# Expert outputs summed from gathered rows, with tokens on partitions, in place of a dense product over all experts

## The chip, the cores and the metric

One core of a Trainium2 chip runs the whole program; the other cores are idle. The metric is the device time of that core in microseconds (us). The kernel before takes 2015.12 us, the median of two runs (2014.29 and 2015.94).

## The reference, cut to what matters

The program is two transformer blocks, one after the other, on 256 tokens of width 1024 in float32. The first block ends with a product-key expert layer (`peer`). It scores 2 x 128 keys in each of 8 heads, takes the best 16 of each half, adds them pairwise, keeps the 16 best pairs, and so chooses 8 x 16 = 128 of 16,384 experts for each token, with a softmax gate for each. An expert is one row of `expert_u` and one row of `expert_v`:

```
u = expert_u[ii]                                   # 128 rows of 1024 for each token
h = jnp.einsum('tkd,td->tk', u, xx).astype(f32)
a = (jax.nn.gelu(h) * gg).astype(x.dtype)
return jnp.einsum('tk,tkd->td', a, expert_v[ii])   # sum over the token's 128 experts
```

The result is added to the residual and normalised. A context norm and the second block (a feed-forward, retention, a Fourier branch, another feed-forward) follow.

## The kernel before, in words

Activations stand with features on the 128 partitions and the 256 tokens along the free axis. A weight comes as a **unit** of 128 x 1024 float32 (512 KB): SP loads it into one of three `raw` buffers, ACT rounds it to `whi` (L108), DVE computes the rest `wlo` (L109), and PE makes three matmuls for each product (L245 to L247). `Emit.run` goes through a list of items, fetches units three ahead, and calls each item in that order; instructions of an engine run in the order in which the items emit them. Items of kind "e" use no weight.

The expert layer has these stages:

- **U stage.** The activations of all 16,384 experts for all tokens are computed densely, in 128 units `pu[b]` (`expert_u`): 24 matmuls, a Gelu on ACT (L1256), and a write of the 128 x 256 result to a DRAM tensor `uD` from the POOL queue (L1257). The choice of the experts (`topk`, `pick`, `gates`) runs on DVE beside the first 64 units.
- **Gate matrix G.** In units 64 to 122 the sparse gates are spread into a dense matrix of 16,384 experts by 256 tokens that stays in SBUF: `gbuild` builds one-hot matrices on DVE, 512 matmuls of 128 x 128 place them (L1243, L1244), and 64 ACT instructions copy them out (L1248).
- **V stage.** In 128 units `pv[b]` (`expert_v`) the gated activations multiply all rows of `expert_v`. For each pair of units POOL loads `early` from `uD` (L1353), DVE multiplies by G (L1383), ACT and DVE split the product into `ah` and `al`, and PE makes 24 matmuls into four accumulating banks `acc`.
- Beside the V stage run eleven `ada` steps: POOL loads a row of 512 KB (L102) and DVE takes its products (L1004). The context norm runs there too. `open_pd` loads the residual `h` back from the tensor `hD` (1 MB) from the POOL queue, two units before the end, and `done_c` adds the four banks to it. The next unit on PE is the context's part of the feed-forward, and then the part that reads `y`, made of the sum.

POOL's DMAs take eight completion semaphores in turn (DMASW0 to DMASW7), so that a DMA waits for the one that stands eight places ahead of it on POOL to have landed.

Of the kernel before, what the change touches and what calls it, by code (L numbers as in the profile page):

```python
# [14 lines left out]
U16 = mybir.dt.uint16  # L15
AF = mybir.ActivationFunctionType
# [11 lines left out]
GSCALE = 16384.0  # L28
# [6 lines left out]
TKE, GB0, GB1 = 63, 64, 58  # L35

NE = 7
# [13 lines left out]
class Emit:  # L51


    def __init__(self, nc, raw, split, ahead_raw, ahead_split):
        self.nc, self.raw, self.split = nc, raw, split
        self.ahead_raw, self.ahead_split = ahead_raw, ahead_split
        self.row, self.ahead_row, self.row_end = None, 0, 0
        self.late, self.soon = [], []

# [27 lines left out]
    def run(self, items, begin=None):  # L87
# [6 lines left out]
        def fetch():  # L94
# [5 lines left out]
            while nr < min(self.row_end, ur + self.ahead_row):  # L100
                rowt[nr] = self.row(nr)
                (nc.scalar if nr < self.ahead_row else nc.gpsimd).dma_start(out=rowt[nr], in_=rows[nr])  # L102
                nr += 1
# [95 lines left out]
def body(ctx, tc, I, out):  # L199
# [40 lines left out]
    uD = dram.tile([P, P, T], F32, name="uD")  # L240
# [784 lines left out]
    i1T = state.tile([P, T], F16, name="i1T")  # L1025
    i2T = state.tile([P, T], F16, name="i2T")
    ghT = state.tile([P, T], F16, name="ghT")
    glT = state.tile([P, T], F16, name="glT")
# [145 lines left out]
    def gates(t):  # L1174

        def a():
            pb = B["p"]
            v = B["vals", t]
            B["ge"] = pb.tile([P, 4, P], F32, name="ge", tag="cand", bufs=1)
            e = B["ge"][:, 0, :].rearrange("p (h k) -> p h k", h=8)  # L1180
# [4 lines left out]
        def b():  # L1185
# [5 lines left out]
            dve.tensor_scalar(out=rc, in0=rc, scalar1=GSCALE, scalar2=None, op0=ALU.mult)  # L1191
            dve.tensor_tensor(out=e, in0=e, in1=rc.unsqueeze(2).to_broadcast([P, 8, 16]), op=ALU.mult)
            e2 = e.rearrange("p h k -> p (h k)")
            h16 = pb.tile([P, P], F16, name="gh16", tag="gh16", bufs=1)
            dve.tensor_copy(h16, e2)
            h32 = B["ge"][:, 1, :]
            dve.tensor_copy(h32, h16)
            l32 = B["ge"][:, 2, :]
            dve.tensor_tensor(out=l32, in0=e2, in1=h32, op=ALU.subtract)
            B["hl"] = (h32, l32)  # L1200

        def c():
            h32, l32 = B["hl"]
            ps = bankB()
            for n, src in enumerate((B["x", 0, t], B["x", 1, t], h32, l32)):
                pe.matmul(ps[:, n * P:n * P + P], src, ident, start=True, stop=True)

            def g():
                for n, dst in enumerate((i1T, i2T, ghT, glT)):
                    dve.tensor_copy(dst[:, t * P:t * P + P], ps[:, n * P:n * P + P])  # L1210
            em.later(g)

        return [(0.5, [("e", None, a)]), (1.5, [("e", None, b)]), (2.0, []), (1.5, [("e", None, c)])]

    NG = 8

    def gbuild(g):

        ts = slice(g * NG, g * NG + NG)
        box = {}  # L1220

        def one_hot():
            pb = B["p"]

            def of(t):

                return t[:, ts].rearrange("p (g t) -> p g t", g=4).unsqueeze(2).to_broadcast([P, 4, P, 2])

            keys = iota.unsqueeze(1).to_broadcast([P, 4, P, 2])
            p1, p2, ph = [pb.tile([P, 4, P, 2], F16, name=n, tag=n, bufs=2) for n in ("p1", "p2", "ph")]  # L1230
            dve.tensor_tensor(out=p1, in0=keys, in1=of(i1T), op=ALU.is_equal)
            dve.tensor_tensor(out=p2, in0=keys, in1=of(i2T), op=ALU.is_equal)
            dve.tensor_tensor(out=ph, in0=p1, in1=of(ghT), op=ALU.mult)
            dve.tensor_tensor(out=p1, in0=p1, in1=of(glT), op=ALU.mult)
            box["t"] = (p2, p1, ph)

        def place(g4):
            p2, p1, ph = box["t"]
            ps = bankB()
            for i in range(4):  # L1240
                o = ps[:, i * P:i * P + P]
                k, t = 2 * g4 + i // 2, i % 2
                pe.matmul(o, p2[:, k, :, t], ph[:, k, :, t], start=True, stop=False)  # L1243
                pe.matmul(o, p2[:, k, :, t], p1[:, k, :, t], start=False, stop=True)  # L1244
            ps3 = ps.rearrange("p (t i) -> p t i", t=4)
            t0 = g * NG + 4 * g4
            o3 = B["G"][:, :, t0:t0 + 4].rearrange("p i t -> p t i")
            em.later(lambda: act.activation(out=o3, in_=ps3, func=AF.Copy, scale=1.0 / GSCALE))  # L1248

        return ("e", None, one_hot), ("e", None, lambda: place(0)), ("e", None, lambda: place(1))  # L1250

    def expert_u(b):

        def ev(ps):
            u = B["pu"].tile([P, T], F32, name="act", tag="act", bufs=2)
            act.activation(out=u, in_=ps[:, :T], func=AF.Gelu_apprx_tanh)  # L1256
            pool.dma_start(out=uD[:, b, :], in_=u)  # L1257
# [55 lines left out]
    gb = {}  # L1313
# [3 lines left out]
    gb[GB0][0:0] = [E(em.flush), E(lambda: open_g())]  # L1317
    gb.setdefault(GB0 + GB1 - 4, []).append(E(lambda: load_early(0)))
    gb[GB0 + GB1 + 3] += [E(em.flush), E(lambda: open_e()), E(lambda: gated(0))]
    gb[GB0 + GB1 + 4] = [E(lambda: ready1(0)), E(em.flush)]  # L1320
    gb[GB0 + GB1 + 5] = [E(lambda: ready1(1))]
# [5 lines left out]
    def open_g():  # L1327

        Bx.close()
        g = Gx.enter_context(tc.tile_pool(name="g", bufs=1))  # L1330
        B["G"] = g.tile([P, P, T], F32, name="G")
        B["pu"] = Gx.enter_context(tc.tile_pool(name="pu", bufs=1))
        C["e", 0] = B["pu"].tile([P, 2, T], F32, name="early0")
        B["p"] = Cgx.enter_context(tc.tile_pool(name="pg", bufs=1))

    def open_e():

        Cgx.close()
        B["pe"] = Gx.enter_context(tc.tile_pool(name="pear", bufs=NE - 1))
        for n in range(1, NE):  # L1340
            load_early(n)

    def part(a, n):

        return B["G"][:, a:a + n, :]
# [4 lines left out]
    def load_early(n):  # L1350
        if n > 0:
            C["e", n] = B["pe"].tile([P, 2, T], F32, name="early", tag="early")
        pool.dma_start(out=C["e", n], in_=uD[:, 2 * n:2 * n + 2, :])  # L1353

    def open_rows():
        K["cs"] = [flat(part(16 + 4 * n, 4)) for n in range(2)]
        K["junk"] = flat(part(24, 4))

    def load_ctx(n):
        pool.dma_start(out=part(40 + 4 * n, 4), in_=I["ctx"][:, 4 * n:4 * n + 4, :])  # L1360

    def load_rows():
        em.rows(lambda n: flat(part(28 + 4 * (n % 3), 4)), 2, ADA_C)
# [3 lines left out]
    def ready(b, a):  # L1367
        ah, al = apair()
        split(a, ah, al)
        C["a", b] = (ah, al)  # L1370

    def ready1(b):
        n = b // 2
        ready(b, C["e", n][:, b % 2, :])
        if b % 2 == 0:
            em.later(lambda: gated(n + 1))
        elif 0 < n and n + NE - 1 < 64:
            load_early(n + NE - 1)

    def gated(n):  # L1380

        if n < 64:
# [717 lines left out]
```

## Time and profile before

| | |
|---|---|
| median of the runs shown | 2015.12 us |
| the profiled execution | 2017.51 us, its span 2015.8 us |
| PE busy | 1990.5 us (99%) |
| DVE, ACT, POOL busy | 1397.2, 1015.9, 152.8 us |
| bytes moved by DMA | 393.18 MB, mean 195 GB/s |
| U stage, V stage (from PE in order of time) | some 248 to 659 us, 659 to 1025 us |

A busy PE is not a PE at its peak, since matmuls overlap: what one costs is the distance between the starts of two, not the duration in its row. The tables by stretch say how busy each engine and the DMA engines are in a stage; the groups say what ended an engine's idle time; the order of time shows distances.

### The profile page before, as it was taken

The page shows a single profiled execution, that of the slowest core. Times are in us where ns is not written, and L with a number is a line of the kernel's source. Part 1 is how long each engine was busy: PE and PEld are TensorE (multiplying, and loading weights), DVE is VectorE, ACT ScalarE, POOL GpSimd, SP SyncE. Part 2 cuts the span into 40 slices and gives each one's busy share as a digit, 9 for nine tenths or more (in the row PEclk, how much of TensorE's full clock was granted, in tenths as well). Part 3 has the DMA queues.
Part 4 walks back from the last instruction along what each step waited for, and adds up shares of the span by engine and source line. Part 5 has one row for each costly group of instructions (what it writes and reads, how often), then busy time and mean ns, then how long its engine had stood idle before and what let it go on. Part 6 is the DMA issues. An engine that isn't in the chain of part 4 may idle for free.

```text
span 2015.8 us, 37798 instructions
## 1 busy us (share of the span) xinstructions
PE 1990.5 (99%) x15348; PEld 1909.2 (95%) x15348; DVE 1397.2 (69%) x2282; ACT 1015.9 (50%) x1510; POOL 152.8 (8%) x296
## 2 busy tenths in 40 slices
PE   9999999999999999999999999999999999999998
PEld 8899999999999999999998888899989999999998
DVE  7668788877676666698876776578654556478555
ACT  6555545456666444545563333345644445346444
POOL 0000011111112101111000001010000000000000
PEclk9999999999999999999999999999999999999999
DMA  7655576766667777887764656677633334455664
GB/s 243 196 162 191 175 226 223 233 197 184 183 184 223 244 235 246 275 293 256 220 221 141 196 194 222 198 236 263 191 123 97 111 107 133 136 172 170 192 185 124
DMA packets 110094, 393.18 MB, mean 195 GB/s; under 512 B 14103, under 2 KB 14487, under 8 KB 109536
## 3 DMA queue, kind: packets, MB, share of 16 engines
q1 hardware_dynamic: 85968, 310.55, 48.8%
q0 software_dynamic: 22944, 77.52, 11.7%
q8 instruction: 120, 1.97, 0.4%
q10 hardware_dynamic: 1008, 2.70, 0.4%
q14 instruction: 54, 0.44, 0.1%
HBM read 371.84 MB, written 18.87 MB: 194 GB/s over the span
## 4 chain that ended last, share of the span: by engine, by line
PE 94%; DVE 2%; DMA 1%; ACT 1%; issue 1%; SPq 0%; ACTq 0%; DVEq 0%; POOLq 0%
PE wk L245 18%; PE wk L246 18%; PE wk L247 18%; PE acc L246 10%; PE acc L245 10%; PE acc L247 10%; PE acc L416 2%; PE acc L417 2%; PE acc L418 2%; DVE wlo L109 1%; PE wk L1243 1%; DMA raw<-w_dram 1%; PE wk L1244 1%; ACT whi L108 0%; ACT G L1248 0%
## 5 line engine op out<-in xcount | busy, mean ns | idle before, releaser
L109 DVE TENSOR_TENSOR wlo<-raw,whi 128x1024 fp32r<-128x1024 f32 x587 | 716.9, 1223 | 507.9 <-ACT whi L108 505.9
L108 ACT CAST whi<-raw 128x1024 fp32r<-128x1024 f32 x587 | 614.7, 1048 | 698.3 <-PE wk L246 338.3
L245 PE MATMUL wk<-nhi,whi 128*128 128x256 f32 (+1 forms) x1744 | 497.1, 285 | 10.3 <-ACT G L1248 10.3
L247 PE MATMUL wk<-nhi,wlo 128*128 128x256 f32 (+1 forms) x1744 | 491.7, 282 | 0.3 <-DVE wlo L109 0.3
L246 PE MATMUL wk<-nlo,whi 128*128 128x256 f32 (+1 forms) x1744 | 489.8, 281 | 0.0
L246 PE MATMUL acc<-al,whi 128*128 128x256 f32 x1376 | 387.9, 282 | 0.1
L247 PE MATMUL acc<-ah,wlo 128*128 128x256 f32 x1376 | 387.7, 282 | 0.0
L245 PE MATMUL acc<-ah,whi 128*128 128x256 f32 x1376 | 387.7, 282 | 0.0
L245 PEld LDWEIGHTS wk<-nhi,whi 128*128 128x128 f32 x1744 | 328.6, 188 | 12.6 <-ACT G L1248 11.7
L246 PEld LDWEIGHTS wk<-nlo,whi 128*128 128x128 f32 x1744 | 329.6, 189 | 0.6 <-issue 0.5
L247 PEld LDWEIGHTS wk<-nhi,wlo 128*128 128x128 f32 x1744 | 329.4, 189 | 0.6 <-DVE wlo L109 0.5
L246 PEld LDWEIGHTS acc<-al,whi 128*128 128x128 f32 x1376 | 259.2, 188 | 1.3 <-DVE al L377 0.5
L245 PEld LDWEIGHTS acc<-ah,whi 128*128 128x128 f32 x1376 | 259.3, 188 | 0.9
L247 PEld LDWEIGHTS acc<-ah,wlo 128*128 128x128 f32 x1376 | 259.3, 188 | 0.0
L246 PE MATMUL wk<-nxl,whi 128*128 128x512 f32 (+1 forms) x544 | 188.5, 346 | 0.0
L245 PE MATMUL wk<-nxh,whi 128*128 128x512 f32 (+1 forms) x544 | 188.2, 346 | 0.0
L247 PE MATMUL wk<-nxh,wlo 128*128 128x512 f32 (+1 forms) x544 | 187.3, 344 | 0.0
L376 ACT CAST ah<-early 128x256 fp32r<-128x256 f32 x128 | 52.1, 407 | 170.2 <-PE acc L247 163.8
L247 PEld LDWEIGHTS wk<-nxh,wlo 128*128 128x128 f32 x544 | 102.2, 188 | 13.2
L245 PEld LDWEIGHTS wk<-nxh,whi 128*128 128x128 f32 x544 | 102.1, 188 | 13.0
L246 PEld LDWEIGHTS wk<-nxl,whi 128*128 128x128 f32 x544 | 102.1, 188 | 11.8
L1257 POOL DMA_DIRECT2D uD<-act x128 | 69.1, 540 | 393.6 <-ACT act L1256 326.0
(534 smaller groups left out, 3215.5 us busy)
## 6 DMA issues: line engine op xcount, KB each, us to landing
raw<-pu_dram SPq DMA_DIRECT2D x128, 512.0 KB, 3.8
raw<-pv_dram SPq DMA_DIRECT2D x128, 512.0 KB, 4.3
row<-ada_dram POOLq DMA_DIRECT2D x59, 512.0 KB, 4.7
raw<-f13a_dram SPq DMA_DIRECT2D x44, 512.0 KB, 3.6
raw<-f2a_dram SPq DMA_DIRECT2D x44, 512.0 KB, 4.2
raw<-f13b_dram SPq DMA_DIRECT2D x44, 512.0 KB, 3.6
raw<-w_dram SPq DMA_DIRECT2D x41, 512.0 KB, 3.9
uD<-act POOLq DMA_DIRECT2D x128, 128.0 KB, 3.9
```

Of the source, the lines that this page charges most:

```text
L108: nc.scalar.copy(hi, r)
L109: nc.vector.tensor_tensor(out=lo, in0=r, in1=hi, op=ALU.subtract)
L245: pe.matmul(o, whi, xhi, start=start, stop=False)
L246: pe.matmul(o, whi, xlo, start=False, stop=False)
L247: pe.matmul(o, wlo, xhi, start=False, stop=stop)
L376: act.copy(hi, src)
L416: pe.matmul(o, xh[:, k, ts], hi[:, sl], start=k == 0, stop=False)
L417: pe.matmul(o, xh[:, k, ts], lo[:, sl], start=False, stop=False)
L418: pe.matmul(o, xl[:, k, ts], hi[:, sl], start=False, stop=k == KD - 1)
L1243: pe.matmul(o, p2[:, k, :, t], ph[:, k, :, t], start=True, stop=False)
L1244: pe.matmul(o, p2[:, k, :, t], p1[:, k, :, t], start=False, stop=True)
L1257: pool.dma_start(out=uD[:, b, :], in_=u)
```

## The change

The matrix G, its one-hot matrices and the dense product with `expert_v` go. The result is summed with tokens on partitions instead, in two halves t of 128 tokens. `gates` computes two tables of numbers per half: `idx` (which expert) and `el` (where in `uD` the activation of that expert for that token lies). For each half and each k of 128 there is a **slot**: one indirect DMA (`row`) fetches for each of the 128 tokens the row of its k-th expert from `expert_v` (512 KB in 128 pieces of 4 KB), and one indirect DMA (`element`) fetches its activation (128 pieces of 4 bytes). For an even k DVE multiplies the row by the gated activation and adds it to `o`; for an odd k ACT makes a diagonal matrix of the activations and PE adds its product with the row in two banks, by two matmuls of full float32. Elements are fetched 32 slots ahead, rows 14 slots ahead, in 16 buffers; the first 14 rows are fetched in the U stage. `back` turns the sums around into `acc` by 16 matmuls. The `ada` rows, the context and the conditioning vectors of this stage are now loaded from the SP queue.

```diff
-TKE, GB0, GB1 = 63, 64, 58
-NE = 7
+TKE = 64
+BEHIND, NROW, AHEAD = 14, 16, 32
...
-    uD = dram.tile([P, P, T], F32, name="uD")
+    uD = dram.tile([P * P, T], F32, name="uD")
...
         def c():
...
+            dve.scalar_tensor_tensor(out=f[0], in0=B["x", 0, t], scalar=float(P), in1=B["x", 1, t], op0=ALU.mult,
+                                     op1=ALU.add)
+            dve.tensor_copy(B["idx", t], f[0])
+            dve.tensor_scalar(out=f[1], in0=f[0], scalar1=float(T), scalar2=None, op0=ALU.mult)
+            dve.tensor_scalar(out=f[1], in0=f[1], scalar1=tok[:, t:t + 1], scalar2=None, op0=ALU.add)
+            dve.tensor_copy(B["el", t], f[1])
...
-    for g in range(T // NG):
-        for n, it in enumerate(gbuild(g)):
-            gb.setdefault(GB0 + g * GB1 // 31 + (0, 2, 3)[n], []).append(it)
...
+    gb = {TKE + 2: [E(em.flush), E(lambda: open_g())]}
+    for n in range(BEHIND):
+        gb[TKE + 4 + 3 * n] = [E(lambda n=n: row(n))]
...
+    def row(n):
+        t, k = divmod(n, P)
+        r = held["r", n] = B["rp"].tile([P, D], F32, name="erow", tag="erow")
+        pool.indirect_dma_start(out=r, out_offset=None, in_=I["pv"].rearrange("a b d -> (a b) d"),
+                                in_offset=at_(B["idx", t], t, k), bounds_check=P * P - 1)
+
+    def element(n):
+        t, k = divmod(n, P)
+        if k % 16 == 0:
+            held["a", n // 16] = B["p"].tile([P, 16], F32, name="ea", tag="ea", bufs=4)
+        pool.indirect_dma_start(out=held["a", n // 16][:, k % 16:k % 16 + 1], out_offset=None,
+                                in_=uD.rearrange("e t -> (e t)").unsqueeze(1), in_offset=at_(B["el", t], t, k),
+                                bounds_check=P * P * T - 1)
+
+    def use(n):
+        t, k = divmod(n, P)
+        a = held["a", n // 16]
+        if k % 16 == 0:
+            dve.tensor_tensor(out=a, in0=a, in1=B["gate", t][:, k:k + 16], op=ALU.mult)
+        r, a, o = held.pop(("r", n)), a[:, k % 16:k % 16 + 1], B["o", t]
+        if k == 0:
+            dve.tensor_scalar(out=o, in0=r, scalar1=a, scalar2=None, op0=ALU.mult)
+        elif k % 2 == 0:
+            dve.scalar_tensor_tensor(out=o, in0=r, scalar=a, in1=o, op0=ALU.mult, op1=ALU.add)
+        else:
...
+            d = B["p"].tile([P, P], F32, name="diag", tag="diag", bufs=4)
+            act.mul(d, ident, a)
+            for i in range(2):
+                pe.matmul(B["po"][i], d, r[:, i * 512:i * 512 + 512], start=k == 1, stop=k == P - 1)
+        if k == P - 1:
+            for i in range(2):
+                oi = o[:, i * 512:i * 512 + 512]
+                dve.tensor_tensor(out=oi, in0=oi, in1=B["po"][i], op=ALU.add)
+
+    def slot(n):
+        if n == 0:
+            for m in range(AHEAD):
+                element(m)
+        if n + AHEAD < 2 * P:
+            element(n + AHEAD)
+        if n + BEHIND < 2 * P:
+            row(n + BEHIND)
+        use(n)
...
+    def back():
+        accp.b = [bankA() for _ in range(4)]
+        for d in range(KD):
+            for t in range(2):
+                pe.matmul(accp.o(d)[:, t * P:t * P + P], B["o", t][:, d * P:d * P + P], ident, start=True, stop=True)
...
+    for n in range(2 * P):
+        items += beside.pop(n, []) + [E(lambda n=n: slot(n))]
+    assert not beside
+    items += [E(back), E(open_pd), E(done_c), E(em.flush)]
```

POOL, where the U stage ends and the V stage begins, before: writes of the activations and loads of `early` for a pair of units (128x512) alternate.

```order
L1257 DMA uD<-act 128x256 [waits DMASW1_49,Activation_49]
L1353 DMA early<-uD 128x512 [waits DMASW2_49,DVE_49,PE_49]
L1353 DMA early<-uD 128x512 [waits DMASW3_49]
...
L1257 DMA uD<-act 128x256 [waits DMASW4_49,Activation_49]
L1353 DMA early<-uD 128x512 [waits DMASW5_49,DVE_49]
L1353 DMA early<-uD 128x512 [waits DMASW6_49,DVE_49]
```

The same place in the changed kernel, where `ea` are the activations of 16 slots and `erow` is a row buffer:

```order
L1210 DMA uD<-act 128x256 [waits DMASW2_49,Activation_49]
L1210 DMA uD<-act 128x256 [waits DMASW3_49,Activation_49]
L1302 DMA ea<-uD,el_181 128x1 [waits DMASW4_49,DMASW5_49,DMASW3_49,DMASW6_49,DMASW2_49,DMASW7_49,DMASW1_49,DMASW0_49]
L1302 DMA ea<-uD,el_181 128x1 x7
L1302 DMA ea<-uD,el_181 128x1 [waits DMASW4_49]
...
L1295 DMA erow<-pv_dram,idx_180 128x1024 [waits DMASW5_49]
L1302 DMA ea<-uD,el_181 128x1 [waits DMASW6_49]
L1295 DMA erow<-pv_dram,idx_180 128x1024 [waits DMASW7_49]
L1302 DMA ea<-uD,el_181 128x1 [waits DMASW0_49]
L1295 DMA erow<-pv_dram,idx_180 128x1024 [waits DMASW1_49,DVE_49]
```

The first element now stands behind the landing of every write to `uD`. Behind it are 33 elements in a row, and then one row and one element in turn, to the end of the stage.

PE, from the last unit of the U stage to the first of the feed-forward, in the changed kernel (`cq` belongs to the context norm):

```order
L248 MATMUL wk<-nhi,wlo 128x256
L1322 MATMUL wk<-erow,diag 128x512 x212
L260 MATMUL wk<-cq_5424,ones 128x256 x2
L1322 MATMUL wk<-erow,diag 128x512 x44
L1354 MATMUL acc<-ident,o_5418 128x128
...
L1354 MATMUL acc<-ident,o_5419 128x128
L246 MATMUL wk<-nhi,whi 128x256
```

256 matmuls of 512 columns and 16 of 128 stand where 3,072 of 256 columns stood.

## Rows read from the trace of the kernel before

**Rows 1.** Page, part 2: the span in 40 slices of 50.4 us.
```profile
PEclk9999999999999999999999999999999999999999
DMA  7655576766667777887764656677633334455664
```

**Rows 2.** Busy time by stretch: second half of the U stage, then the V stage.
```profile
core 0: us, PE busy (x) PEld busy (x) DVE busy (x) ACT busy (x) POOL busy (x), PEclk, DMA share, GB/s
434.00:659.00 225.00, 214.74 (x2031) 210.90 (x2030) 153.34 (x191) 144.82 (x192) 37.47 (x70) 1.00 0.64 194
659.00:1025.00 366.00, 365.91 (x3078) 365.40 (x3078) 279.37 (x387) 189.05 (x280) 43.37 (x81) 1.00 0.78 253
```

**Rows 3.** PE in order of time (start, duration): the V stage's first matmul, and the first after it.
```profile
658.95 0.28 PE L245 MATMUL acc<-ah,whi 128*128 128x256 f32 x1
...
1024.99 0.28 PE L245 MATMUL wk<-nhi,whi 128*128 128x256 f32 x1
```

**Rows 4.** PE groups of 434 to 659 us: busy, mean ns, idle before.
```profile
L245 PE MATMUL wk<-nhi,whi 128*128 128x256 f32 x508 | 147.2, 290 | 10.3 <-ACT G L1248 10.3
```

**Rows 5.** PE in order of time: one placing (eight matmuls) between two units.
```profile
630.74 0.23 PE L1243 MATMUL wk<-ph,p 128*128 128x128 f16 x1
...
631.18 0.36 PE L245 MATMUL wk<-nhi,whi 128*128 128x256 f32 x1
631.39 0.28 PE L246 MATMUL wk<-nlo,whi 128*128 128x256 f32 x1
```

**Rows 6.** POOL groups of the whole span: busy, mean ns, idle before.
```profile
L1353 POOL DMA_DIRECT2D early<-uD x64 | 34.3, 537 | 277.1 <-DVE al L377 277.1
L612 POOL IOTA iota<- 128x256 f16 x1 | 1.5, 1512 | 0.4 <-POOLq L2086 0.4
```

**Rows 7.** Tile uD: its writes (ns min/median/max), issue to landing of all its DMAs.
```profile
L1257 POOL DMA_DIRECT2D uD<-act x128: 539/539/548, 252.0 to 662.2; - x128
...
DMA to landing us min/median/max: 1.9/3.9/7.8
```

**Rows 8.** POOL in order of time: six loads back to back.
```profile
647.38 3.19 POOL L1353 DMA_DIRECT2D early<-uD  x6
```

**Rows 9.** DMA of the V stage: slices, queue (packets, MB, share), issues (landing).
```profile
GB/s 230 230 237 232 236 223 227 235 238 236 223 227 246 222 293 270 278 308 216 348 226 295 295 298 283 291 278 301 280 295 217 237 223 241 215 220 207 177 201 364
...
q1 hardware_dynamic: 18268, 66.50, 54.9%
...
G<-ada_dram POOLq DMA_DIRECT2D x11, 512.0 KB, 6.6
raw<-f13a_dram SPq DMA_DIRECT2D x4, 512.0 KB, 9.2
...
G<-cc_dram POOLq DMA_DIRECT2D x2, 512.0 KB, 7.1
```

**Rows 10.** DVE groups of the V stage.
```profile
L109 DVE TENSOR_TENSOR wlo<-raw,whi 128x1024 fp32r<-128x1024 f32 x128 | 156.7, 1224 | 56.0 <-ACT whi L108 55.1
...
L1004 DVE CUSTOM_DVE_ANT_0 G<-G,vec 128x1024 f32<-128x1024 f32 x22 | 28.1, 1278 | 0.0
```

**Rows 11.** Tile G: its matmuls of full float32, two instructions to each.
```profile
L259 PE MATMUL wk<-G,ones x4: 379/379/379, 967.2 to 967.8; 128*128 128x256 f32 x4
```

**Rows 12.** Page, part 6: an issue of the POOL queue, us to landing.
```profile
row<-ada_dram POOLq DMA_DIRECT2D x59, 512.0 KB, 4.7
```

**Rows 13.** DVE in order of time behind the V stage; then the load of tile h.
```profile
1028.02 2.73 DVE L1429 TENSOR_TENSOR h<-acc,h 128x256 f32<-128x256 f32 x8
1030.66 3.26 DVE L290 SCALAR_TENSOR_TENSOR y<-h,gain,y 128x256 fp32r<-128x256 f32 x8
...
DMA to landing us min/median/max: 6.9/6.9/6.9
```

More of the change, by code (lines that the diff above doesn't have):

```diff
@@ L101, in fetch @@
                 rowt[nr] = self.row(nr)
-                (nc.scalar if nr < self.ahead_row else nc.gpsimd).dma_start(out=rowt[nr], in_=rows[nr])
+                (nc.scalar if nr < self.ahead_row else self.row_queue).dma_start(out=rowt[nr], in_=rows[nr])
                 nr += 1
@@ L1213, in gates @@
-        return [(0.5, [("e", None, a)]), (1.5, [("e", None, b)]), (2.0, []), (1.5, [("e", None, c)])]
[L1215 to L1250, printed above, removed]
@@ L1329, in open_g @@
         Bx.close()
[L1330 to L1341, printed above, removed]
@@ L1343, in part @@
-    def part(a, n):
-        return B["G"][:, a:a + n, :]
+        p = B["p"] = B["pu"] = Gx.enter_context(tc.tile_pool(name="pv", bufs=1))
+        B["rp"] = Gx.enter_context(tc.tile_pool(name="rp", bufs=NROW))
+        for t in range(2):
+            B["o", t] = p.tile([P, D], F32, name=f"o{t}")
+        K["cs"] = [p.tile([P, 1024], F32, name=n) for n in ("csx1", "csc1")]
+        K["junk"] = p.tile([P, 1024], F32, name="junk1")
+        C["x"] = p.tile([P, KD, T], F32, name="ctx1")
+        C["q"] = [p.tile([P, 512], F32, name=f"cq{j}") for j in range(4)]
@@ new lines, in use @@
+    def use(n):
[9 more added lines that the diff above has]
+        else:
+            if k == 1:
+                B["po"] = [bankB() for _ in range(2)]
+            d = B["p"].tile([P, P], F32, name="diag", tag="diag", bufs=4)
[6 more added lines that the diff above has]
+                dve.tensor_tensor(out=oi, in0=oi, in1=B["po"][i], op=ALU.add)
@@ L1355, in open_rows @@
[L1355 to L1360, printed above, removed]
     def load_rows():
-        em.rows(lambda n: flat(part(28 + 4 * (n % 3), 4)), 2, ADA_C)
+        load_cs(nc.sync)
+        nc.sync.dma_start(out=C["x"], in_=I["ctx"])
+        em.row_queue = nc.sync
+        em.rows(lambda n: B["p"].tile([P, 1024], F32, name="row1", tag="row1", bufs=3), 2, ADA_C)
@@ L1365, in body @@
     accp = Acc()
[L1367 to L1382, printed above, removed]
-            dve.tensor_tensor(out=C["e", n], in0=C["e", n], in1=part(2 * n, 2), op=ALU.mult)
-    def expert_v(b):
-        def fn(hi, lo):
-            ah, al = C.pop(("a", b))
-            accp.step(hi, lo, ah, al, b == 0, b == P - 1)
-            if b == P - 1:
-                done_c()
-            elif b < P - 2:
-                em.soon.append(lambda: ready1(b + 2))
-        return fn
+    def back():
+        accp.b = [bankA() for _ in range(4)]
+        for d in range(KD):
+            for t in range(2):
+                pe.matmul(accp.o(d)[:, t * P:t * P + P], B["o", t][:, d * P:d * P + P], ident, start=True, stop=True)
```

81 lines of the change are left out of this document (21 added, 60 removed).

## The prediction, made before the changed kernel had run

> **What bounds the kernel now.** I read the slices first: the granted TensorE clock stays at the top of its two levels to the end [rows 1]. The table by stretch comes next. From 659 to 1025 us PE is busy 365.91 of 366.00 us, and DVE only 279 [rows 2]. The V stage's first matmul starts at 658.95 us and the first matmul behind it at 1024.99 [rows 3]: 366 us for 128 units, 2.86 us each, or 119 ns from one of the 24 matmuls to the next. So the V stage lasts as long as PE needs for a dense product. The stretch before it is PE's too, with 214.74 of 225.00 us [rows 2]; the 10.3 us that PE stood idle there ended with the ACT copies of G [rows 4]. POOL is busy 37 and 43 us in the two stretches [rows 2]: it is idle now, and the change gives it the whole stage.
>
> **What goes.** The V stage, 366 us. In the second half of the U stage PE computes 508 / 8 = 63.5 units [rows 4], which at 2.86 us are 182 us; the other 43 of the 225 us belong to G. They are 64 placings of 0.44 us, 28 us, from the first matmul of one to the unit behind it [rows 5]; the 10.3 us of idle time; and about 6 us in which the first matmul behind a placing runs 0.21 instead of 0.12 us [rows 5]. In all 409 us go from the profiled execution's 2017.51 us, and 1608.5 us remain, to which the new V stage is added. The change breaks even where that stage takes 409 us, from the end of the U stage to where the feed-forward starts as it did.
>
> **What comes, on POOL.** Behind the U stage POOL issues 256 element DMAs and 256 - 14 = 242 row DMAs, 498 in a row. No row shows an indirect DMA. A direct one costs POOL 539 ns [rows 7], and six back to back take 3.19 us, 0.53 each [rows 8]. That is the lower end, since an indirect DMA writes as many descriptors and must also read 128 offsets from 128 partitions. The upper end is the slowest POOL instruction of the trace that touches all partitions, the iota with 1.51 us [rows 6]. I take two passes over 128 entries, one to read offsets and one to write descriptors, 2 x 0.53 = 1.06 us: it is nearest to the row of the same work, and a second pass is what the word indirect adds. So 498 x 1.06 = 530 us, with 265 and 753 us at the ends. By the Trainium skill (DMA: Bandwidth & Descriptors, Anatomy of one DMA) descriptor generation is a small part of a DMA's fixed cost, and many descriptors go out before it shows; by that rule the lower end would hold, and the first rival below would be the outcome.
>
> **What comes, on the DMA engines.** 242 rows of 0.524 MB are 127 MB. With eleven ada rows, the two conditioning vectors, four weights ahead [rows 9] and the context of 1 MB, which counts twice, 19 more loads of 0.524 MB make it 137 MB. Queue q1 moved 66.50 MB in 54.9% of 16 engines' 366 us, which is 331 GB/s while its packets ran [rows 9]: 413 us. The best slice of the stage reached 348 GB/s [rows 9]: 393 us. The 4-byte pieces of an element DMA lie between nothing and the time of 4 KB pieces, 1.6 us a DMA at that rate. Time goes with bytes wherever the rows show it, so I take 0.1 us, 26 us in all. 413 + 26 = 439 us is below 530, so the transfers hide behind POOL; a landing of some 5 us [rows 12] also fits in the eight POOL instructions of 1.06 us until its semaphore is used again.
>
> **What comes on the others lies below POOL.** PE: 128 odd slots with two float32 matmuls of 512 columns. Those of 256 columns are two instructions each and start 0.2 us apart [rows 11], so a matmul of 512 takes 0.8 us and the stage 205 us; at the lower level of the clock, 1.2 GHz, 410 us. DVE: 128 products of 128 x 1024 at the 1.22 us of the same shape in the row for `wlo`, 157 us, and the ada steps' 28 us as before [rows 10]. ACT: 128 diagonals of 128 x 128, under half a microsecond each. If POOL were not there, PE at the lower clock and the DMA engines would come next, at nearly the same time.
>
> **What comes at the ends.** At the start the first element waits for the last write of `uD`: the Gelu, the issue of 0.54 us and 3.9 us to landing [rows 7], 5 us. The elements that follow are part of the 498. At the end: the last row's landing, 4.7 us [rows 12]; its product on PE, 1.7; two DVE additions, 1.4; 16 float32 matmuls of `back`, some 3.3 (half of the 0.2 us of [rows 11] for each of 32 instructions). Then the load of `h`, which stood two units ahead of the end and now stands behind the last row: 0.5 + 6.9 us, where the additions used to start 3.0 us after the last matmul [rows 3, 13], so 4.4 us more. Sum 15.5 us.
>
> The new stage is 5 + 530 + 15.5 = 550.5 us, and the program 1608.5 + 550.5 = 2159 us by the profiled execution, which lies 2.4 us above the median: 2157 us, 7% slower. Moving the ada rows and context to SP's queue costs nothing: SP has no weights to load in this stage but the few ahead, and POOL's 530 us is the cover. Fourteen rows in the U stage cost PE nothing either, while POOL is busy a sixth of that time.
>
> **Rivals.**
> - The DMA engines are the bound: an indirect issue costs little more than a direct one, 0.53 to 0.8 us. Then the stage is 5 + 439 + 15.5 = 459.5 us and the program 2066 us; at the 348 GB/s of the best slice and with free elements, 2020 us. For it speaks that the direct issue takes the same 0.54 us for loads of 256 KB [rows 6] and writes of 128 KB [rows 7]; against it, that these read no table. Half of this case lies within 2%.
> - POOL is locked out by DVE. Half the slots have a DVE product with two inputs in SBUF, 1.22 us. If POOL can't read its offsets meanwhile, 128 x 1.22 = 157 us are added to the forecast: 2314 us. Against it: POOL's direct DMAs never took more than 548 ns [rows 7], though DVE ran `wlo`, also with two inputs, for 157 of 366 us [rows 10]; but these have no offsets to read. The Trainium skill (SBUF — State Buffer, Who interferes with whom) says that such a DVE instruction blocks a GpSimd instruction that reads SBUF, and not one that only writes it. The trace agrees with the second half, and no row here shows the first.
> - Faster: issues at most 0.70 us, and rows that come in faster than any slice of the stage. The point is 2% below the median, 1975 us, a stage of 369 us: 348 us for 137 MB, 393 GB/s. At 400 GB/s the stage takes 5 + 342 + 15.5 us and the program 1969 us. For it: q0 would have the engines almost to itself, and the slice of 348 GB/s had them not wholly busy. Against it: nothing in the stage has held 300 GB/s for long [rows 9].
>
> **How the numbers follow.** 2% is about what a measurement of this kernel can tell from no change. Slower by 2% begins at 2055 us, a stage of 449 us, an issue of 0.86 us. Chances: issue-bound from 0.86 us up 0.50; DMA-bound 0.26, half of it slower and half within 2%; locked out 0.12; faster 0.07; issues between 0.78 and 0.86 us, within 2%, 0.05. So slower 0.75, within 2% 0.18, faster 0.07. The range goes from 2010 us, which leaves out the faster case and a little of the DMA-bound one, to 2330 us, an issue of 1.41 us, which leaves out half of the lock case and the longest issues.
>
> **What would show it.** An indirect DMA on POOL of 1.06 us and POOL near fully busy from the end of the U stage to the last row: right. POOL idle before its row DMAs, waiting for DMA landings, with DMA slices near 350 GB/s: the first rival. POOL durations that stretch beside DVE's products: the second. U units 2.86 us apart to the end would show the 43 us, and PE idle between its last slot and the feed-forward's `y` the end term. The forecast fails if an issue is under 0.8 us, or if element pieces take much more than 0.1 us a DMA, which would add to either case.

## The result, and the profile after

The changed kernel takes 2321.9 us (median of two runs, 2320.4 to 2323.4) where the kernel before took 2015.1: a ratio of 1.152, with an interval of 1.150 to 1.155. The forecast was 2157 us. The sign was right and the time lay inside the range, but the loss is 307 us where 142 were expected. The profiled execution took 2320.40 us, with a span of 2318.7.

The page's slices of the whole span, to be held against [rows 1]:

```profile
PE   9999999999555555555555799999999999999998
POOL 0000111232377777777777600010100000000000
PEclk9999999999866777767667899999999999999999
DMA  7556577788536666766666646666864333445654
GB/s 239 183 173 194 196 231 229 260 293 270 193 87 195 208 206 206 227 189 190 189 190 181 246 154 192 198 209 191 279 216 154 110 102 109 128 153 176 190 186 128
```

For twelve slices of 58 us PE is half busy, POOL is at seven tenths (gaps do not count as busy), and the DMA engines move about 200 GB/s with a share near six tenths, once rows are fetched again (the second of the twelve slices, with 87 GB/s, has elements alone). By stretch, with the columns of [rows 2], the first half of the new stage and the second:

```profile
core 0: us, PE busy (x) PEld busy (x) DVE busy (x) ACT busy (x) POOL busy (x), PEclk, DMA share, GB/s
647.00:980.00 333.00, 184.62 (x248) 60.60 (x246) 99.70 (x101) 26.11 (x64) 260.15 (x240) 0.71 0.63 194
980.00:1316.00 336.00, 194.50 (x257) 62.95 (x257) 100.20 (x107) 32.65 (x81) 262.85 (x241) 0.70 0.66 199
```

No engine is busy all the time: POOL, the busiest, has 260 of 333 us. What fills the rest is seen only in order of time. This is POOL and DVE in the middle of the stage (start, duration, and in brackets the idle time before it and what ended that):

```profile
799.80 1.01 POOL L1302 DMA_INDIRECT ea<-uD,el  x1 [0.30 <-issue]
800.46 1.28 DVE L1315 SCALAR_TENSOR_TENSOR o<-erow,ea,o 128x1024 f32<-128x1024 f32 x1 [4.47 <-DMA erow<-pv_dram,idx]
801.12 1.51 POOL L1295 DMA_INDIRECT erow<-pv_dram,idx  x1 [0.30 <-issue]
802.94 1.01 POOL L1302 DMA_INDIRECT ea<-uD,el  x1 [0.30 <-DMA erow<-pv_dram,idx]
804.25 1.01 POOL L1295 DMA_INDIRECT erow<-pv_dram,idx  x1 [0.30 <-issue]
805.56 1.01 POOL L1302 DMA_INDIRECT ea<-uD,el  x1 [0.31 <-issue]
806.29 1.28 DVE L1315 SCALAR_TENSOR_TENSOR o<-erow,ea,o 128x1024 f32<-128x1024 f32 x1 [4.55 <-DMA erow<-pv_dram,idx]
806.88 1.58 POOL L1295 DMA_INDIRECT erow<-pv_dram,idx  x1 [0.30 <-issue]
```

Two things are to be read here. An indirect issue takes 1.01 us, and in front of each one POOL stands still for 0.30 us, mostly without any event that the profile shows as the end of a wait ("issue"). Where a row's issue begins while a DVE product runs, it is longer: the product of 800.46 ends at 801.74, and the issue that began at 801.12 ends at 802.63. The issue of 799.80, which had begun before the product, is not stretched. Over the whole chain 121 issues begin while such a product runs, and 108 of them last over 1.1 us; of the 115 during which a product begins, one does. DVE and PE, for their part, wait for rows.

The chain of issues runs from 623.20 to the end of the last row's issue. The lines show it from the last matmul of the U stage to the feed-forward:

```profile
613.17 0.28 PE L248 MATMUL wk<-nhi,wlo 128*128 128x256 f32 x1
617.19 0.54 POOL L1210 DMA_DIRECT2D uD<-act  x1 [4.51 <-ACT act L1209]
623.20 1.09 POOL L1302 DMA_INDIRECT ea<-uD,el  x1 [5.47 <-DMA uD<-act]
...
1315.91 1.00 POOL L1295 DMA_INDIRECT erow<-pv_dram,idx  x1 [0.30 <-issue]
1323.67 0.69 DVE L1326 TENSOR_TENSOR o<-o,wk 128x512 f32<-128x512 f32 x1 [1.92 <-PE wk L1322]
...
1327.82 0.36 PE L246 MATMUL wk<-nhi,whi 128*128 128x256 f32 x1
...
1328.69 0.69 POOL L1368 DMA_DIRECT2D h<-hD  x1 [11.77 <-DVE w L1374]
...
1334.02 2.74 DVE L1391 TENSOR_TENSOR h<-acc,h 128x256 f32<-128x256 f32 x8 [1.66 <-DMA h<-hD]
```

That is 693.7 us for 498 issues, 1.39 us each. All 497 gaps are 0.30 us and make 151.5 us; the durations make 542.2 us, of which 38.3 are what 112 issues of over 1.1 us took beyond the usual 1.01. Behind the first, no issue waited for a buffer. The groups of the page say it in sums (busy, mean ns, idle before):

```profile
L1295 POOL DMA_INDIRECT erow<-pv_dram,idx x256 | 295.5, 1154 | 78.3 <-issue 72.2 <-DMA erow<-pv_dram,idx 3.4 <-PE wk L1322 1.8
L1302 POOL DMA_INDIRECT ea<-uD,el x256 | 262.1, 1024 | 83.2 <-issue 69.5 <-DMA erow<-pv_dram,idx 7.9 <-DMA uD<-act 5.5
L1315 DVE SCALAR_TENSOR_TENSOR o<-erow,ea,o 128x1024 f32<-128x1024 f32 x126 | 161.9, 1285 | 462.7 <-DMA erow<-pv_dram,idx 462.5
```

The account closes. The last write of `uD` is issued at 617.19 where it stood at 662.2 [rows 7], 45.0 us earlier. From there to the feed-forward's first matmul it is 1327.82 - 617.19 = 710.6 us, and it was 1024.99 - 662.2 = 362.8 [rows 3, 7]. The difference, less the 45.0, is 302.8 us; the two profiled executions lie 302.9 us apart. Behind that matmul both kernels need the same time to the end, 990.9 and 990.8 us.

### The profile page after: what moved, and what is told of

It is laid out like the page before. It is cut to its first block, busy times and chain, and to the rows that moved or that the text cites. A ratio compares the mean times of both kernels' runs of the same rounds, so it can differ in the third digit from the quotient of the medians.

```text
span 2318.7 us, 32229 instructions
## 1 busy us (share of the span) xinstructions
PE 1977.3 (85%) x12292; PEld 1641.3 (71%) x12292; DVE 1244.5 (54%) x1976; ACT 830.4 (36%) x1318; POOL 669.6 (29%) x730
## 5 line engine op out<-in xcount | busy, mean ns | idle before, releaser
L110 DVE TENSOR_TENSOR wlo<-raw,whi 128x1024 fp32r<-128x1024 f32 x459 | 560.7, 1224 | 490.3 <-ACT whi L109 489.1
L109 ACT CAST whi<-raw 128x1024 fp32r<-128x1024 f32 x459 | 480.8, 1049 | 703.3 <-PE wk L247 367.9
L1322 PE MATMUL wk<-erow,diag 128*128 128x512 f32 x512 | 384.8, 897 | 325.4 <-DMA erow<-pv_dram,idx 277.5
L1322 PEld LDWEIGHTS wk<-erow,diag 128*128 128x128 f32 x512 | 125.2, 269 | 583.9 <-issue 467.4
L1315 DVE SCALAR_TENSOR_TENSOR o<-erow,ea,o 128x1024 f32<-128x1024 f32 x126 | 161.9, 1285 | 462.7 <-DMA erow<-pv_dram,idx 462.5
L1295 POOL DMA_INDIRECT erow<-pv_dram,idx x256 | 295.5, 1154 | 78.3 <-issue 72.2
L1302 POOL DMA_INDIRECT ea<-uD,el x256 | 262.1, 1024 | 83.2 <-issue 69.5
L1320 ACT ACTIVATE diag<-ident,ea 128x128 f32<-128x128 f32 x128 | 47.5, 397 | 609.2 <-DVE ea L1310 301.5
L103 POOL DMA_DIRECT2D row<-ada_dram x59 | 31.3, 531 | 416.2 <-DVE modx L1005 400.1
```

What stands on the lines that cost most here:

```text
L103: (nc.scalar if nr < self.ahead_row else self.row_queue).dma_start(out=rowt[nr], in_=rows[nr])
L109: nc.scalar.copy(hi, r)
L110: nc.vector.tensor_tensor(out=lo, in0=r, in1=hi, op=ALU.subtract)
L1295: pool.indirect_dma_start(out=r, out_offset=None, in_=I["pv"].rearrange("a b d -> (a b) d"), in_offset=at_(B["idx", t], t, k), bounds_chec ...
L1302: pool.indirect_dma_start(out=held["a", n // 16][:, k % 16:k % 16 + 1], out_offset=None, in_=uD.rearrange("e t -> (e t)").unsqueeze(1), in ...
L1315: dve.scalar_tensor_tensor(out=o, in0=r, scalar=a, in1=o, op0=ALU.mult, op1=ALU.add)
```

## The experiments

Three theories stood. **Issue**: the stage lasts as long as POOL needs for 498 indirect issues, 1.32 us each with the gap. **Transfers**: it lasts as long as the DMA engines need for 137 MB in pieces of 4 KB and 4 bytes. **Lock**: DVE's products with two inputs in SBUF hold up POOL's reading of the offsets. The chain that the text speaks of runs from the first issue behind the U stage to the end of the last. All columns but the first two are read from the one profiled execution of each kernel.

| kernel | us | ratio to before (interval) | chain, us | issue, us | issues over 1.1 us (excess) | gaps over 0.4 us (excess) |
|---|---|---|---|---|---|---|
| changed | 2321.9 | 1.152 (1.150 to 1.155) | 693.7 | 1.013 | 112 (38.3) | none |
| no elements, 242 issues | 1982.2 | 0.984 (0.981 to 0.987) | 355.2 | 1.007 | 58 (37.6) | none |
| half rows | 2359.6 | 1.171 (1.168 to 1.173) | 736.0 | 1.015 | 120 (79.7) | none |
| even sums in PSUM | 2324.0 | 1.153 (1.151 to 1.155) | 701.2 | 1.012 | 14 (5.4) | 32 (39.7) |
| no bounds check | 2325.1 | 1.154 (1.151 to 1.156) | 698.5 | 0.947 | 100 (45.1) | 13 (28.9) |
| all slots on DVE, PSUM | 2325.5 | 1.154 (1.152 to 1.156) | 695.1 | 1.011 | 10 (4.9) | 37 (34.2) |
| the same, no bounds check | 2337.9 | 1.160 (1.158 to 1.162) | 699.7 | 0.943 | 12 (5.6) | 59 (71.9) |
| half the offsets of the elements | 2334.8 | 1.158 (1.156 to 1.161) | 702.4 | 0.957, 1.020 | 99 (39.6) | 18 (19.7) |
| no products | 2293.0 | 1.138 (1.128 to 1.147) | 659.9 | 1.010 | 6 (5.7) | none |
| no products, no bounds check | 2303.3 | 1.143 (1.140 to 1.146) | 671.2 | 0.947, then 1.095 | 10 (5.4) | 2 (1.1) |
| all slots on PE | 2302.4 | 1.141 (1.137 to 1.145) | 660.7 | 1.010 | 11 (6.1) | none |

**The elements left out.** Their 256 DMAs are gone and constants stand in their place; the rows and the sums stay.

```
-        pool.indirect_dma_start(out=held["a", n // 16][:, k % 16:k % 16 + 1], ..., in_offset=at_(B["el", t], t, k), ...)
+        if k % 16 == 0:
+            act.copy(held["a", n // 16], ident[:, 0:16])
```

> Leaves out the 256 element DMAs (constants stand in their place). Issue theory: the stage is a chain of POOL issues, each 1.01 us and 0.30 us to the next, some stretched. 256 of the 498 go, so 242 x 1.46 = 353 us remain of 694 and the program takes about 1980 us, unless 137 MB at 331 GB/s (413 us) end later, then about 2040 us. Transfer theory (the DMA engines are the bound, and POOL waits for them): only the 4-byte pieces go, at most 100 us, so 2220 us or more.

1982.2 us: 340 us went with 256 DMAs that carry 512 bytes each, 1.33 us for each, which is its issue and its gap. By transfers alone at most 100 us should have gone, so that theory falls as the bound of the changed kernel. It is next in line, though:

```profile
640.00:975.00 335.00, 235.24 (x473) 84.74 (x473) 185.47 (x195) 54.93 (x150) 265.52 (x229) 0.96 0.99 375
```

The DMA engines are busy 0.99 of this kernel's stage and move 375 GB/s, which no slice of the V stage before had shown [rows 9].

**Half the bytes of each row.** A row brings 2 KB, and the sums use each half row twice; the count of DMAs is the same.

```
-        pool.indirect_dma_start(out=r, ..., in_=I["pv"].rearrange("a b d -> (a b) d"), ...)
+        pool.indirect_dma_start(out=r, ..., in_=I["pv"].rearrange("a b (c d) -> (a b c) d", c=2), ...)
```

> Fetches half a row (2 KB instead of 4 KB) for each token and slot and uses it twice; the number of DMAs stays. Issue theory: no change, 2322 us within 1%. Transfer theory: 63 MB less, 190 us at 331 GB/s, so about 2130 us.

2359.6 us, 1.6% slower than the changed kernel with about half its bytes. Transfers are out as the bound. What was not foreseen is the loss of 38 us, and the groups show it:

```profile
L1302 POOL DMA_INDIRECT ea<-uD,el x256 | 331.5, 1295 | 83.4 <-issue 72.8 <-DMA uD<-act 5.7 <-DMA ea<-uD,el 3.7
L1295 POOL DMA_INDIRECT erow<-pv_dram,idx x256 | 268.4, 1048 | 78.3 <-issue 69.7 <-DMA erow<-pv_dram,idx 6.1 <-PE wk L1325 1.2
```

Now it is the element issues that are long, on average 1295 ns where they were 1024. A half row lands at another moment of POOL's turn, so DVE's product meets another issue, and holds it up longer: 79.7 us in all, 41 more than before, about the difference of the chains. Of the 120 long issues 114 begin during a DVE product and end 0.88 to 0.90 us after it, as those of the changed kernel do: that is the lock with the timing moved.

**Even sums in PSUM.** Each even product is done in two halves of 512 columns on a sum that stays in PSUM, so that DVE has one input in SBUF.

```
-            dve.scalar_tensor_tensor(out=o, in0=r, scalar=a, in1=o, op0=ALU.mult, op1=ALU.add)
+                    dve.scalar_tensor_tensor(out=w, in0=q, scalar=a, in1=w, op0=ALU.mult, op1=ALU.add)
```

> DVE's products of the even slots are summed in PSUM instead of SBUF, so that they have one SBUF input instead of two; all else stays. Lock theory: the row DMAs that last 1.5 instead of 1.01 us do so because POOL waits for a DVE product with two SBUF inputs; without them every issue takes 1.01 us, 498 x 0.076 = 38 us less, 2284 us. Rival (the longer issues come from the row's own descriptors or from full rings): POOL durations as before, 2322 us.

The long issues fall from 112 to 14 and their excess from 38.3 to 5.4 us, as the lock wants it. The time did not follow, 2324.0 us: 32 gaps appeared that are longer than 0.4 us. POOL in order of time:

```profile
807.66 1.01 POOL L1302 DMA_INDIRECT ea<-uD,el  x1 [0.30 <-issue]
809.81 1.01 POOL L1295 DMA_INDIRECT erow<-pv_dram,idx  x1 [1.13 <-issue]
811.12 1.01 POOL L1302 DMA_INDIRECT ea<-uD,el  x1 [0.30 <-issue]
813.31 1.01 POOL L1295 DMA_INDIRECT erow<-pv_dram,idx  x1 [1.17 <-issue]
```

**No bounds check**, in either of the two DMAs.

```
-                                in_offset=at_(B["idx", t], t, k), bounds_check=P * P - 1)
+                                in_offset=at_(B["idx", t], t, k))
```

> Takes the bounds check out of both indirect DMAs, and with it the register that POOL loads for each. If the 0.30 us between two indirect DMAs are that register's load and the check is part of the 1.01 us: up to 498 x 0.30 = 150 us less, 2170 us. If the 0.30 us belong to every indirect DMA: 2322 us within 1%.

An issue takes 0.947 instead of 1.013 us and the gap stays: the check costs 66 ns, and the gap belongs to the indirect DMA itself. Again the 33 us saved came back: 28.9 us in 13 gaps of up to 4.7 us, and 7 us in longer stretches. At one of these gaps ACT, POOL and PE resume together, behind an event that the view calls "remote":

```profile
925.98 1.28 DVE L1314 SCALAR_TENSOR_TENSOR o<-erow,ea,o 128x1024 f32<-128x1024 f32 x1 [4.19 <-DMA erow<-pv_dram,idx]
928.29 0.40 ACT L1319 ACTIVATE diag<-ident,ea 128x128 f32<-128x128 f32 x1 [10.10 <-remote]
928.48 0.94 POOL L1295 DMA_INDIRECT erow<-pv_dram,idx  x1 [4.62 <-remote]
928.74 0.50 PEld L1321 LDWEIGHTS wk<-erow,diag 128*128 128x128 f32 x2 [8.29 <-ACT diag L1319]
```

In the kept trace the signal that ends ACT's and POOL's wait is PE's own, for a finished product; it comes 6.2 us after the end of the last product recorded. Whether the signal or the record is late is not shown.

**Direct DMAs for both**: same bytes, pieces, buffers and order, but addresses fixed by the program.

```
-        pool.indirect_dma_start(out=r, out_offset=None, in_=I["pv"]..., in_offset=at_(B["idx", t], t, k), ...)
+        pool.dma_start(out=r, in_=I["pv"][n % P])
...
+        pool.dma_start(out=held["a", n // 16][:, k % 16:k % 16 + 1], in_=uD[k * P:k * P + P, t:t + 1])
```

> Both the rows and the elements of the V stage are fetched by direct DMAs from POOL in place of the indirect ones: the same bytes, pieces, buffers and order, but addresses that the program fixes, so not the experts that the gates chose. It prices the word indirect. In the changed kernel an issue with its gap costs 1.32 us (1.013 + 0.30), in the same program a direct one 0.53 to 0.54 us with no gap behind it. Theory one, that the price is in the indirect issue on POOL: 498 x 0.54 = 269 us would be POOL's part, the stage is then set by the transfers, which needed at most 355 us with the elements left out, and by PE; 2321.9 - 694 + 355 to 440 = 1983 to 2070 us, and the gap of 0.30 us is gone. Theory two, that 498 DMAs of any kind through POOL's queue cost that much: about 2320 us, with the gap still there. The lock: a direct issue reads no offsets, so none is stretched beside DVE's products.

2018.0 us, 1.0013 times the kernel before (1.0002 to 1.0023), near the 2020 us that the first rival of the prediction gave at 348 GB/s and with free elements. POOL in order of time, and the table by stretch:

```profile
643.63 0.54 POOL L1301 DMA_DIRECT2D ea<-uD  x1
644.45 0.54 POOL L1295 DMA_DIRECT2D erow<-pv_dram  x1 [0.28 <-issue]
644.97 0.54 POOL L1301 DMA_DIRECT2D ea<-uD  x1
...
630.00:1010.00 380.00, 253.39 (x492) 91.51 (x490) 195.25 (x204) 57.63 (x143) 251.90 (x474) 0.94 0.94 338
```

An issue costs 0.54 us as in [rows 7], the elements without a gap, and the DMA engines are the bound with 0.94 of the time. In front of the rows POOL stands idle for 122 us in all, 71 of it until a landing; 39 us are called "issue", like the 0.28 above, so that this kernel does not tell whether a direct row has a gap of its own. The six direct loads of [rows 8] have none. So what costs 304 us in the changed kernel is that the addresses come from a table; some 5 of them are the wait for `uD`, since the first direct element is issued 0.5 us behind the last write, not 6.0.

**Elements direct, rows indirect.** One of the two edits above.

> Rows by indirect DMAs as in the changed kernel, elements by direct ones (the same bytes and pieces, but addresses that the program fixes, so not the chosen ones). If the price belongs to each indirect DMA for itself: 242 x (1.013 + 0.30) + 256 x 0.54 = 456 us, and some 40 us for the stretch beside DVE's products, so 456 to 496 us in place of 694 and 2084 to 2124 us. If the price comes from the two kinds in turn: with the gap of 0.30 us gone everywhere, 242 x 1.013 + 256 x 0.54 = 383 us and about 2010 us; with a gap behind every DMA, 533 us and 2160 us.

2149.7 us, 1.067 times before (1.063 to 1.071). POOL in order of time:

```profile
809.95 0.56 POOL L1302 DMA_DIRECT2D ea<-uD  x1
810.82 1.07 POOL L1295 DMA_INDIRECT erow<-pv_dram,idx  x1 [0.30 <-issue]
811.89 0.56 POOL L1302 DMA_DIRECT2D ea<-uD  x1
812.75 1.07 POOL L1295 DMA_INDIRECT erow<-pv_dram,idx  x1 [0.30 <-issue]
```

The 0.30 us stand in front of each indirect DMA; the direct element follows without a gap. So the price goes with each indirect DMA, and the kinds do not need to alternate for it. The chain of 526 us lies near the 533 of a gap behind every DMA, but the rows rule that out. The time is 26 us above the 2084 to 2124 expected: here both kinds take 4 to 6% longer, 0.56 and 1.07 us, 92 long issues add 46 us, and a few waits 6. What makes both of POOL's kinds of issue longer in this kernel was not found.

**Elements for 64 partitions of 128**, constants for the others.

```
-        ... out=held["a", n // 16][:, k % 16:k % 16 + 1], ..., in_offset=at_(B["el", t], t, k)
+        ... out=held["a", n // 16][0:64, k % 16:k % 16 + 1], ..., ap=B["el", t][0:64, k:k + 1]
```

> The element DMAs fetch for 64 of the 128 partitions; the other 64 get constants from ACT. Number of DMAs and everything else as in the changed kernel. It tells whether an indirect issue's 1.013 us go with the offsets or are fixed. Per offset: 256 issues of about 0.55 us in place of 1.01, 118 us less, 2204 us. Fixed: unchanged 1.01 us and 2322 us. My prediction's picture of two passes over 128 entries is the first of the two.

```profile
L1304 POOL DMA_INDIRECT ea<-uD,el x256: 942/957/1737, 633.9 to 1307.0; - x128
```

Half the offsets save 56 of 1013 ns (minimum, median and maximum stand in the row): 0.9 ns for an offset, some 0.9 us that are fixed. The picture of two passes over 128 entries is wrong. The time is 2334.8 us, since the chain came to 702.4 us with 18 new gaps, and began 10.7 us later (the U stage ended later in this execution).

**All slots on DVE, sums in PSUM; the same without the bounds check.** ACT's diagonals and PE's products fall away.

```
-        if k % 2 == 0:
             for i in range(2):
                 w, q = B["do"][i], r[:, i * 512:i * 512 + 512]
...
-            act.mul(d, ident, a)
```

> All 256 slots are summed by DVE, each product in two halves of 512 columns on sums that stay in PSUM; PE's odd products and ACT's diagonals fall away. The bounds check stays. DVE then needs 256 x 2 x 0.75 = 385 us, less than POOL's chain. It tests why the kernel with PSUM sums alone gained nothing although its stretched issues fell from 112 to 14: new gaps of 1 to 5 us stood before POOL's issues. If these come from ACT and PE falling behind with the odd slots and so holding row buffers, they are gone here: chain 498 x (1.013 + 0.30) = 654 us + 5 of stretch, 2321.9 - 35 = 2287 us. If they come from late landings or from POOL itself, they stay: chain near 700, 2322 us. If DVE becomes the bound: no, unless its product from PSUM takes over 1.3 us.

> The same with the bounds check left out of both indirect DMAs, which took 66 ns from each issue and was given back in gaps before. If ACT and PE were what gave it back: chain 498 x (0.947 + 0.305) = 623 us, 2321.9 - 694 + 623 = 2251 us, 3% below the changed kernel. If the gaps have another source: 2290 to 2325 us.

2325.5 and 2337.9 us. The guess that ACT and PE with the odd slots had caused the gaps falls: they are there without them. In the second of the two POOL's issues and gaps make 2.50 us a slot. DVE there, in order of time:

```profile
829.76 0.76 DVE L1318 SCALAR_TENSOR_TENSOR acc<-erow,ea,acc 128x512 f32<-128x512 f32 x1 [1.59 <-remote]
831.15 0.75 DVE L1318 SCALAR_TENSOR_TENSOR acc<-erow,ea,acc 128x512 f32<-128x512 f32 x1 [0.64 <-DVE acc L1318]
833.25 0.75 DVE L1318 SCALAR_TENSOR_TENSOR acc<-erow,ea,acc 128x512 f32<-128x512 f32 x1 [1.35 <-DVE acc L1318]
834.64 1.47 DVE L1318 SCALAR_TENSOR_TENSOR acc<-erow,ea,acc 128x512 f32<-128x512 f32 x2 [0.64 <-issue]
```

Starts lie 1.39, 2.10 and 1.39 us apart, near multiples of 0.70, also where no DMA is named as what a half waits for. DVE falls behind, holds the row buffers, and POOL waits for them.

**No products.** Both indirect DMAs stay, and nothing uses what they bring; once with the bounds check and once without. The sums are constants.

```
     def use(n):
...
-        r, a, o = held.pop(("r", n)), a[:, k % 16:k % 16 + 1], B["o", t]
...
+        held.pop(("r", n))
+        if k == 0:
+            dve.tensor_copy(B["o", t].rearrange(...), ident.unsqueeze(1).to_broadcast(...))
```

> Both indirect DMAs stay as in the changed kernel, 498 in the stage, bounds check and all, but nothing uses what they fetch: the gate product, DVE's and PE's products and ACT's diagonals are left out (the sums are constants). Issue theory with the lock: without DVE's products no issue is stretched and no buffer is held, so the chain is 498 x (1.013 + 0.30) = 654 us, 40 us below the 694 of the changed kernel. If a second limit of about 1.40 us for each indirect DMA stands behind POOL's issue (five kernels whose issues alone would have taken 623 to 660 us ended at 695 to 702), the chain is near 695 again, with gaps before the issues though nothing holds a buffer. The time is 2275 us by the first and 2315 us by the second.

> The same without the bounds check, so an issue of 0.947 + 0.305 us. Issue theory: 498 x 1.252 = 623 us, about 2245 us. A limit of 1.40 us behind POOL: near 695 us again and about 2315 us. Between the two it would say that the engines that use the rows, not the fetching, gave back what the earlier kernels saved.

With the check (2285.1 and 2300.8 us in two runs): the tile's row again as minimum, median and maximum.

```profile
L1295 POOL DMA_INDIRECT erow<-pv_dram,idx x256: 999/1009/1115, 438.2 to 1281.3; - x128
```

The longest row issue is 1.12 us and the chain is 659.9 us, where 654 were expected: 498 x 1.010 + 497 x 0.30 + 5.7. So no limit of 1.40 us stands behind POOL, and 34 us of the changed kernel's chain go with the products. The chain is that of the execution of 2285.1 us; what made the other 15.7 us longer is not shown. Without the check the chain is 671.2 us and not 623. Most of the first 212 issues came 1.25 us apart as expected, and then the duration changed at one stroke, though nothing used the rows:

```profile
891.03 0.95 POOL L1295 DMA_INDIRECT erow<-pv_dram,idx  x1 [0.30 <-issue]
892.28 1.07 POOL L1302 DMA_INDIRECT ea<-uD,el  x1 [0.30 <-issue]
893.65 1.10 POOL L1295 DMA_INDIRECT erow<-pv_dram,idx  x1 [0.30 <-issue]
895.05 1.10 POOL L1302 DMA_INDIRECT ea<-uD,el  x1 [0.30 <-issue]
```

272 issues of 1.09 to 1.10 us follow, 1.40 us from one to the next, again twice 0.70, and behind them nine of 0.94 us.

**All slots on PE**, with ACT's diagonals; DVE keeps the gate product.

```
-        if k == 0:
-            dve.tensor_scalar(out=o, in0=r, scalar1=a, scalar2=None, op0=ALU.mult)
-        elif k % 2 == 0:
-            dve.scalar_tensor_tensor(out=o, in0=r, scalar=a, in1=o, op0=ALU.mult, op1=ALU.add)
-        else:
...
+                pe.matmul(B["po"][i], d, r[:, i * 512:i * 512 + 512], start=k == 0, stop=k == P - 1)
```

> All 256 slots are summed by PE with ACT's diagonals, as the odd ones are in the changed kernel; DVE keeps only the gate product of every 16 slots. So no DVE product with two inputs in SBUF stands beside POOL's issues, and both indirect DMAs and the bounds check stay. The lock: the stretched issues fall from 112 to about 10 and the chain goes from 694 to the 654 to 660 us of the kernel without products, so 2280 to 2290 us, if PE keeps up. PE needs 4 x 0.59 = 2.4 us a slot at the full clock, and POOL gives it one every 2.63 us: it keeps up at 2.4 GHz. If it is granted the lower level, a slot takes 3.78 us and PE is the bound: 256 x 3.78 = 968 us, 2590 us. If the saving is given back in gaps before POOL's issues as in the kernels with sums in PSUM, 2315 to 2325 us again.

The chain is 660.7 us with no long gap, 33 us shorter, as the lock theory says, in a kernel that computes the whole. The two halves of its stage:

```profile
647.00:980.00 333.00, 244.31 (x501) 89.26 (x502) 21.48 (x40) 54.11 (x131) 256.49 (x252) 0.96 0.62 195
980.00:1300.00 320.00, 243.62 (x503) 87.56 (x502) 20.43 (x43) 58.45 (x142) 244.12 (x239) 0.99 0.67 212
```

PE has more to do than in the changed kernel, and its granted clock is 0.96 and 0.99 where it was 0.71 and 0.70; its matmuls of 512 columns keep to 0.6 us. The time is 2302.4 us, 19.5 less than the changed kernel and with intervals that do not meet. Of the 33 us, 13 are missing in the profiled execution because the first element was issued at 635.9 us instead of 623.2: the U stage ended later. ACT's Gelus had waited 66 us for writes of `uD` to land, 12 in the changed kernel. Another 7 are missing because it is 17.6 us from the last row's issue to the feed-forward instead of 10.9. The profiled execution of 2307.3 us is so 13.1 below that of the changed kernel. The U stage's code is the same, and what delayed it is open; the four executions of this kernel lie between 2292.6 and 2309.1 us. It beats the changed kernel and not the kernel before.

## Why the prediction was wrong

- **The sign and the mechanism were right**: POOL's issues set the stage, transfers and PE lie below them, and DVE costs only what its hold on POOL's issues adds. Break-even was put at 409 us for the stage.
- **The term that failed is 498 x 1.06 = 530 us**, "the 498 indirect issues". It measured 693.7 us, 164 more, which is nearly the whole miss: 2159 + 164 = 2323 beside the 2320.4 of the profiled execution. In its parts: 498 x 1.012 = 504 us of durations (26 less than the 530, to which the product, 528, had been rounded, and for another reason: a nearly fixed price, not two passes), 151.5 us of gaps that the sum had put at nothing, and 38.3 us of stretch. I had read "no gap" from six direct loads back to back [rows 8], and a direct load is the wrong witness: in front of each indirect one POOL stands still for 0.30 us. 1.39 us for each is nearer to the upper end that I had set, 1.51 from the iota [rows 6], than to 1.06.
- **The lock is real and smaller than its rival's 157 us.** It costs 33 to 38 us of the chain, shown by the two kernels without DVE's products. That the measured time lies 8 us from this rival's 2314 is chance: most of the miss is the gap. The price was wrong in that a product holds an issue up only if it is running when the issue begins, and then for what is left of it: 112 issues, 0.34 us each. Of these, 108 begin during a product, and all 108 end 0.88 to 0.90 us after it. The Trainium skill (SBUF — State Buffer, Who interferes with whom) says that a DVE instruction with two inputs in SBUF contends with a GpSimd instruction that reads SBUF, and not with one that only writes it. The trace now agrees with the first half: PSUM sums, with one input in SBUF, took the long issues from 112 to 14. The direct DMAs of [rows 7], at most 548 ns, agree with the second half; that it is the reading of the offsets that waits is argued from them and not seen by itself. The 548 ns are those of `uD`'s writes, and not, as the prediction has it, of all of POOL's direct DMAs: four others of the kernel before took 551 to 679 ns.
- **The first rival** (DMA engines the bound) has the right size and the wrong condition: with direct DMAs the stage is theirs, and 2018 us came out against its 2020. That the two are so near is in part luck: the best slice of [rows 9] is not 348 but 364 GB/s, the last one, which would have given 2003 us, and the direct kernel held 338. The Trainium skill (DMA: Bandwidth & Descriptors, Anatomy of one DMA) has descriptor generation as a small part of a DMA's fixed cost. That agrees with the direct ones, an issue of 0.54 us where a write of `uD` lands after 3.7 (median), and not with the indirect ones, 1.01 us behind 0.30 of standstill where an element lands after 3.3. My 413 us for 137 MB were too many: the kernel without elements brought the rows in a chain of 355 us. It hid below POOL either way.
- **The other terms were small, and their errors cancel.** The 43 us of G were 45.0 from one last write of `uD` to the other. From the U stage's last matmul to the first element it is 9.7 us, forecast 5: the last write was issued 3.7 us behind the matmul, and POOL then waited 5.47 us for the landing. From the last row's issue to the feed-forward's first matmul it is 10.9 us; forecast were 11.1, and 4.4 for the load of `h`. The additions of `h` do start 6.2 us behind that matmul instead of 3.0 [rows 3, 13], but this cost nothing, since both kernels need the same time from there. PE's granted clock was 0.70 on average, between its two levels of 1.2 and 2.4 GHz, after PE had stood idle behind the U stage; it cost nothing, since PE waited for rows.

## What to carry to other kernels

A gather by indirect DMAs is priced by their count: here 1.32 us of POOL for each, nearly whatever it carries (4 bytes or 4 KB a partition, 64 offsets or 128). So multiply the count by the full distance from one issue's start to the next, and take that distance from a kernel that has indirect DMAs, never from direct ones. And keep DVE instructions with two SBUF inputs away from the start of such issues; PE did the same sums here without being the bound.

## What was not expected

- The gap of 0.30 us in front of every indirect DMA, also without a bounds check, and not in front of the direct element loads. The bounds check itself is 66 ns.
- What the shorter issues saved came back in five kernels: even sums in PSUM, no bounds check, half the offsets, and DVE alone with and without the check had chains of 695 to 702 us, where their issues and gaps alone make 620 to 660. Of the 159 gaps over 0.4 us in these five, 146 stand in front of a row, which needs a free row buffer, and 13 in front of an element: so POOL mostly waits, it seems, for an engine that still holds a row. Why that engine is late is open; the traces of these five lack part of the engines' signals. It is no common limit, since the kernel without products and the one with all slots on PE ran at 1.33 us an issue throughout. In parts of these chains an engine's starts lie on multiples of 0.70 us: DVE without the check, and POOL itself without products and check (1.40 us, 272 times). What sets that step is open, and so is why the signals behind "remote" come late. Fetching several columns of elements with one indirect DMA was not tried.
